# gMLP stage of a two-layer trunk: v ahead of u, the mixing matrix's two parts side by side, and the mixes between units of u

## The chip, the cores and the metric

The kernel runs on one core of a Trainium2 chip. The metric is the device time of one execution in microseconds (us). Of the kernel before, three runs took 1134.57 to 1136.39 us, with a median of 1135.93.

## The reference

The program computes a trunk of two layers on 512 tokens by 1024 channels: layer 0 mixes tokens by stick-breaking attention, layer 1 by a gated MLP, and each mixer is followed by a SwiGLU network (FFN). The change touches layer 1's mixer alone:

```
def token_mixing_mixer(h, w_in, ln_g, w_s, b_s, w_out):
    uv = jax.nn.gelu(h @ w_in)
    u, v = jnp.split(uv, 2, axis=-1)
    v = layer_norm(v, ln_g)
    ...
    ws = jnp.where(chunk_causal[None], w_s, 0.0).astype(v.dtype)
    sv = jnp.einsum('gts,bnsgc->bntgc', ws, v) + b_s.T[None, None, :, :, None]
    y = u * sv.reshape(B, S, D)
    return y @ w_out
```

There are 8 groups g of 128 channels, each with a mixing matrix of 128 positions by 128, and n counts 4 chunks of 128 tokens. So the mixing is 32 products of 128x128 by 128x128.

## The kernel before, in words

**Products in two parts.** A float32 operand is kept as a high part and a low part (`split`, L113: ScalarE rounds to the high part, VectorE subtracts for the low one). A product is three matmuls (`mm3`, L105): high by high, high by low, low by high, added up in one PSUM bank. A bank holds 128 x 512 float32. Six banks go round under one tag ("b"), and two more under a second one ("p").

**Order.** The PE's instructions run in the order in which the program was scheduled. Weights come as raw blocks of 512 KB through the SP queue, in the order of the list that `wadd` fills (L244); each is split into `wh` (ScalarE, L161) and `wl` (VectorE, L162) some units ahead of its use (`wget`, L235).

**Around the stage.** `out_proj` (L497) of FFN 0 ends in the boundary of each block of 128 tokens (`boundary`, L425): residual sum, two norms, 8 transposes on PE into `tp`, and the split into `hTh` and `hTl`, the transposed input of the next sub-layer. The transposes of blocks 2 and 3 must wait for a long chain on VectorE and ScalarE, so PE is given other work there: three closures `nxt`, of which the first runs before block 2's transposes, the second before block 3's, the third behind them. Before, these are `u_first` (L1324): units 0 and 1, units 2 and 3, and unit 4 of u, each for the first 256 tokens.

**The stage** (`gmlp`, L1331). A u unit m (`u_unit`, L1302) makes 128 channels of u for n tokens: 24 matmuls of 256 columns for 256 tokens, 48 for 512; ScalarE then applies GELU (L1315). v is made in two halves of 512 channels, each half in four banks (one for each token block), 24 matmuls of 512 columns a bank (L1345). In order:

1. load and split of the mixing matrices (`wsh`, `wsl`), load of the bias `bsb`; units 0 to 4 of u for tokens 256 to 511
2. v half 0, v half 1; into these `bg.step` deals out pieces of the next modulation's work (class `Bg`, L341), which end in 8 matmuls `adaps` with a matrix of ones, whose operand is split by ScalarE (`acch`) and VectorE (`accl`) just before
3. layer norm of v: statistics and normalising on VectorE, split into `vnh`, `vnl`; units 5 to 7 of u for all tokens stand on PE meanwhile
4. eight mixes (`mix`, L1393), one for each group: 12 matmuls of 128 columns into one bank `sv`, one VectorE instruction svt = sv * gain + bias of 512 columns, one u * svt, and the split of that product (`act_split`, L1043: `as` by ScalarE, then VectorE). From the fifth on, each is followed by `part(m - 4)` (L1415): 12 matmuls `y` of 512 columns, the output projection for token blocks 0 and 3, which take four banks
5. the rest of the projection, `out_proj` with its boundary

Of the kernel before, what the change touches and what calls it, by code (L numbers as in the profile page):

```python
# [13 lines left out]
P = 128  # L14
T = 512
# [16 lines left out]
def trunk(ctx: ExitStack, tc: tile.TileContext, A: dict, out: bass.AP):  # L32
# [21 lines left out]
    def slot(dt, name, a=2, b=512):  # L54
        return s4.tile([P, a, b], dt, tag="s4", name=nm(name))

    def bank(name, tag="b"):
        return psum.tile([P, 512], F32, tag=tag, bufs=6 if tag == "b" else 2, name=nm(name))
# [51 lines left out]
    def load(dst, src):  # L110
        nc.sync.dma_start(out=dst, in_=src)

    def split(hi, lo, src, hi_dve=False):  # L113
        if hi_dve:
            dve.tensor_copy(hi, src)
        else:
            act.activation(hi, src, AF.Copy)  # L117
        dve.tensor_tensor(lo, src, hi.bitcast(F32), ALU.subtract)
# [116 lines left out]
    def wget(src, look=3):  # L235

        n = taken[0]
        taken[0] += 1
        while len(got) < min(n + 1 + look, len(stream)):
            wemit()  # L240
        assert stream[n][3] == src, (stream[n][3], src)
        return got[n]

    def wadd(key, a, b, *idx):  # L244
        ap = A[key]
        stream.append((ap[idx], a, b, (key,) + idx))

    NH = 3
    NU = 5
    wadd("wv", 2, 512, 0, 0)  # L250
    wadd("wqk", 8, P, 0, 0)
    wadd("wqk", 8, P, 0, 1)
# [9 lines left out]
    for l in range(2):  # L262
        for f in range(NH):
            wadd("wgu", 8, P, l, f, 0)
            wadd("wgu", 8, P, l, f, 1)
        for f in range(NH, KF):
            stream.append((None, 0, 0, ("blocks", (l, f - NH))))
        if l == 1:
            for q in range(2):
                for p in PAIRS[q]:  # L270
                    wadd("wdn", 4, 256, q, p)
        if l == 0:
            for f in range(KF):
                wadd("wdown", 1, D, f)
            for m in range(NU):
                wadd("win_u", 8, P, m)
            for hf in range(2):
                for j in range(4):
                    wadd("win_v", 2, 512, hf, j)
            for m in range(NU, KD):  # L280
                wadd("win_u", 8, P, m)
            for k in range(KD):
                wadd("wout", 1, D, k)
# [1018 lines left out]
    def u_unit(hT, m, lo, n, w):  # L1302
        ub = bank("u")
        for k in range(KD):
            for c in range(0, n, 256):
                h, l = hB(hT, k, lo + c, 256)
                mm3(
                    ub[:, c : c + 256], w[0][:, k, :], w[1][:, k, :], h, l,
                    k + c == 0, k == KD - 1,
                )  # L1310

        def evac():
            if m // 2 == len(u4):
                u4.append(slot(F32, "u"))
            last_act[0] = act.activation(  # L1315
                u4[m // 2][:, m % 2, lo : lo + n], ub[:, :n], AF.Gelu_apprx_tanh
            )

        return evac

    uw = {}
    STEPS = 2

    def u_first(hT, ms):  # L1324
        ev = []
        for m in ms:
            uw[m] = wget(("win_u", m), 1)
            ev.append(u_unit(hT, m, 0, 256, uw[m]))
        return lambda: [e() for e in ev]

    def gmlp(bg, hT, nhT, nS, nxt):  # L1331
        wsr = wraw.tile([P, KD, P], F32, tag="raw", name="wsr")
        load(wsr[:], A["ws"])
        nc.gpsimd.memset(wsr[0:64, :, 64:P], 0.0)
        wsh = slot(F32R, "wsh", KD, P)
        wsl = slot(F32R, "wsl", KD, P)
        split(wsh[:], wsl[:], wsr[:])
        bsb = slot(F32, "bsb", KD, P)
        load(bsb[:].rearrange("p a b -> p (a b)"), A["bs"].to_broadcast([P, D]))
        for m in range(NU):  # L1340
            u_unit(hT, m, 256, 256, uw[m])()
        vt = [slot(F32, "vt", 1, 1024) for _ in range(NT)]
        vn = []

        def v_mm(vb, tt, k, w):  # L1345
            a, b = hB(hT, k, tt * P, P)
            mm3(vb[tt][:], a, b, w[0][:, k % 2, :], w[1][:, k % 2, :], k == 0, k == KD - 1)

        def v_gelu(vb, tt, hf):
            act.activation(  # L1350
                vt[tt][:, 0, hf * 512 : (hf + 1) * 512], vb[tt][:], AF.Gelu_apprx_tanh
            )

        vb = [bank("v") for _ in range(NT)]
        for k in range(KD):
            if k % 2 == 0:
                wv = wget(("win_v", 0, k // 2))
            for tt in range(NT):
                v_mm(vb, tt, k, wv)
            bg.step(STEPS)  # L1360
        for tt in range(NT):
            v_gelu(vb, tt, 0)
        vb = [bank("v") for _ in range(NT)]
        for k in range(4):
            if k % 2 == 0:
                wv = wget(("win_v", 1, k // 2))
            for tt in range(NT):
                v_mm(vb, tt, k, wv)
            bg.step(STEPS)
        bg.step(99)  # L1370
        tail = [wget(("win_v", 1, j)) for j in (2, 3)]
        st = small.tile([P, NT, 2, 6], F32, tag="bns", bufs=1, name=nm("bns"))
        mv = small.tile([P, NT, 2], F32, tag="mv", bufs=1, name=nm("mv"))
        for tt in range(NT):
            for k in range(4, KD):
                v_mm(vb, tt, k, tail[k // 2 - 2])
            v_gelu(vb, tt, 1)
            for hf in range(2):
                dve.bn_stats(st[:, tt, hf, :], vt[tt][:, 0, hf * 512 : (hf + 1) * 512])
            dve.bn_aggr(mv[:, tt, :], st[:, tt, :, :])  # L1380
        sd = small.tile([P, 52], F32, tag="sd4", bufs=1, name=nm("sd4"))[:, :NT]
        act.activation(sd, mv[:, :, 1], AF.Sqrt, bias=epsb[:])
        r = small2.tile([P, 48], F32, tag="r4", bufs=1, name=nm("r4"))
        dve.reciprocal(r[:, :NT], sd)
        for tt in range(NT):
            dve.tensor_scalar(
                vt[tt][:, 0, :], vt[tt][:, 0, :], mv[:, tt, 0:1], r[:, tt : tt + 1],
                ALU.subtract, ALU.mult,
            )
            vn.append((slot(F32R, "vnh", 1, 1024), slot(F32R, "vnl", 1, 1024)))  # L1390
            split(vn[tt][0][:, 0, :], vn[tt][1][:, 0, :], vt[tt][:, 0, :])

        def mix(m):  # L1393
            um = u4[m // 2][:, m % 2, :]
            sv = bank("sv")
            for n in range(NT):
                mm3(
                    sv[:, n * P : (n + 1) * P],
                    vn[n][0][:, 0, m * P : (m + 1) * P], vn[n][1][:, 0, m * P : (m + 1) * P],
                    wsh[:, m, :], wsl[:, m, :], True, True,  # L1400
                )
            t = fpool.tile([P, 768], F32, tag="e", name=nm("svt"))[:, :T]
            dve.scalar_tensor_tensor(
                t.rearrange("p (n t) -> p n t", n=NT),
                sv[:].rearrange("p (n t) -> p n t", n=NT), lng[:, m : m + 1],
                bsb[:, m : m + 1, :].to_broadcast([P, NT, P]), ALU.mult, ALU.add,
            )
            dve.tensor_tensor(um, um, t, ALU.mult)

        for m in range(NU, KD):  # L1410
            u_unit(hT, m, 0, T, wget(("win_u", m)))()
        sp = []
        pre = {"w": [], "y": {0: [None, None], 3: [None, None]}}

        def part(k):  # L1415

            w = wget(("wout", k), 2)
            pre["w"].append(w)
            for tt, y in pre["y"].items():
                for hf in range(2):  # L1420
                    if k == 0:
                        y[hf] = bank("y", "p" if tt == 3 else "b")
                    c = slice(hf * 512, (hf + 1) * 512)
                    tok = slice(tt * P, (tt + 1) * P)
                    mm3(
                        y[hf][:], sp[k][0][:, tok], sp[k][1][:, tok],
                        w[0][:, 0, c], w[1][:, 0, c], k == 0, False,
                    )

        for m in range(KD):  # L1430
            mix(m)
            sp.append(act_split(u4[m // 2][:, m % 2, :]))
            if m >= 4:
                part(m - 4)
        out_proj(
            2, KD, lambda k: sp[k], lambda k: ("wout", k), 4, bg, nhT, nxt, pre, nS,
        )
# [9 lines left out]
    bg2 = Bg("A2", "B2", lag=1, gap=3)  # L1447
    f0.run(
        Bg("G1", slots=1), Bg("A1", "B1", "G2"), bg2, 2, hT2,
        [lambda a=a: u_first(hT2, range(a, min(a + 2, NU))) for a in range(0, NU, 2)],  # L1450
    )
    gmlp(bg2, hT2, hT3, S3, f1.first())
    f1.last(Bg("G3", slots=1))
# [101 lines left out]
```

## Time and profile before

| what | us |
|---|---|
| median of three runs (range) | 1135.93 (1134.57 to 1136.39) |
| the profiled execution's own time | 1133.95 |
| its span | 1132.2 |
| PE busy (share of span) | 1110.9 (98%) |
| weight loads on PE | 999.9 (88%) |
| VectorE busy | 933.0 (82%) |
| ScalarE busy | 596.6 (53%) |
| the stage: first transposes of block 3 to the first boundary of its output | 643.85 to 768.71 |

Times within the execution count from the span's start. The profile names an instruction by its line, its engine, and output<-inputs by the program's names. A matmul's bar on PE is longer than the time it takes from its neighbours, since matmuls overlap: the distance from start to start is what a matmul costs. The mean granted clock of TensorE was 0.998.

### The profile page before, as it was taken

How to read it: one execution, taken by the hardware profiler on the slowest of the kernel's cores; microseconds unless marked ns; L12 is line 12 of the kernel's file. 1: busy time of each engine (PE TensorE's matmuls, PEld its weight loads, DVE VectorE, ACT ScalarE, POOL GpSimd, SP SyncE). 2: the span in 40 equal slices, each digit the busy share in tenths (PEclk: the TensorE clock that was granted, in tenths of full speed). 3: DMA queues.
4: the chain of work that ended last, by engine and by line, in shares of the span. 5: the costliest groups of instructions: out<-in, count | busy, mean ns of one | idle time of the engine just before them, and what ended most of it. 6: DMA issues, size and time to landing. Idle time of an engine off the chain costs nothing.

```text
span 1132.2 us, 18659 instructions
## 1 busy us (share of the span) xinstructions
PE 1110.9 (98%) x7436; PEld 999.9 (88%) x7436; DVE 933.0 (82%) x1223; ACT 596.6 (53%) x985; POOL 29.5 (3%) x53
## 2 busy tenths in 40 slices
PE   6999999999999999999999999999999999999997
PEld 4787878788999999998888988988999999999996
DVE  4988999958989898778686865759979898789996
ACT  6445655656655555572153624537455555465752
POOL 0120100000000000010000100001000000000000
PEclk9999999999999999999999999999999999999999
DMA  8876434214344343348886483324243434223242
GB/s 322 336 238 213 147 98 134 93 59 158 122 150 131 128 151 117 129 136 310 269 275 218 150 280 110 131 94 160 83 132 115 164 130 146 70 85 99 90 154 106
DMA packets 51356, 176.39 MB, mean 156 GB/s; under 512 B 6074, under 2 KB 9146, under 8 KB 51268
## 3 DMA queue, kind: packets, MB, share of 16 engines
q1 hardware_dynamic: 48708, 166.81, 43.6%
q0 software_dynamic: 2560, 8.39, 2.0%
q8 instruction: 58, 0.95, 0.3%
q14 instruction: 30, 0.25, 0.1%
HBM read 164.69 MB, written 8.39 MB: 153 GB/s over the span
## 4 chain that ended last, share of the span: by engine, by line
PE 88%; DVE 5%; ACT 3%; DMA 2%; issue 1%; SPq 0%; DVEq 0%; ACTq 0%
PE r L94 32%; PE y L94 16%; PE v L94 8%; PE pqk L94 7%; PE X L94 4%; PE gu L94 4%; PE Y L94 3%; PE u L94 3%; PE av L94 2%; PE z L94 2%; PE tw L102 1%; PE Z L94 1%; PE W L94 1%; PE tp L102 1%; PE ab L94 1%
## 5 line engine op out<-in xcount | busy, mean ns | idle before, releaser
L94 PE MATMUL r<-Sh,wl 128*128 128x256 f32 x608 | 170.0, 280 | 0.0
L94 PE MATMUL r<-Sh,wh 128*128 128x256 f32 x608 | 169.9, 279 | 0.0
L94 PE MATMUL r<-Sl,wh 128*128 128x256 f32 x608 | 169.8, 279 | 0.0
L161 ACT ACTIVATE wh<-raw 128x1024 fp32r<-128x1024 f32 x87 | 91.6, 1059 | 113.3 <-PE y L94 57.5
L94 PE MATMUL y<-wh,as 128*128 128x512 f32 x480 | 150.7, 391 | 0.0
L117 ACT ACTIVATE wh<-f 128x1024 fp32r<-128x1024 f32 x87 | 92.3, 1061 | 91.3 <-PE r L94 66.4
L70 DVE TENSOR_TENSOR wl<-f,wh 128x1024 fp32r<-128x1024 f32 x87 | 106.4, 1222 | 38.9 <-ACT wh L117 38.8
L162 DVE TENSOR_TENSOR wl<-raw,wh 128x1024 fp32r<-128x1024 f32 x87 | 105.8, 1221 | 38.2 <-ACT wh L161 37.5
L94 PEld LDWEIGHTS r<-Sl,wh 128*128 128x128 f32 x608 | 114.2, 188 | 0.0
L94 PEld LDWEIGHTS r<-Sh,wl 128*128 128x128 f32 x608 | 114.2, 188 | 0.0
L94 PEld LDWEIGHTS r<-Sh,wh 128*128 128x128 f32 x608 | 114.1, 188 | 0.0
L94 PEld LDWEIGHTS y<-wh,as 128*128 128x128 f32 x480 | 90.1, 188 | 18.6
L94 PE MATMUL y<-wl,as 128*128 128x512 f32 x240 | 93.8, 391 | 0.0
L94 PE MATMUL r<-hTh,wh 128*128 128x256 f32 x304 | 88.9, 293 | 0.6 <-DVE gu L70 0.6
L94 PE MATMUL r<-hTl,wh 128*128 128x256 f32 x304 | 84.8, 279 | 0.0
L94 PE MATMUL r<-hTh,wl 128*128 128x256 f32 x304 | 80.0, 279 | 0.0
L94 PEld LDWEIGHTS r<-hTh,wh 128*128 128x128 f32 x304 | 57.0, 188 | 5.9 <-DVE gu L70 2.4
L94 PE MATMUL r<-hTh,b 128*128 128x256 f32 x304 | 59.8, 279 | 0.0
L117 ACT ACTIVATE wh<-rawx 128x1024 fp32r<-128x1024 f32 x38 | 40.3, 1061 | 33.4 <-PE r L94 30.8
L94 PEld LDWEIGHTS r<-hTl,wh 128*128 128x128 f32 x304 | 57.2, 188 | 0.1
L94 PEld LDWEIGHTS r<-hTh,wl 128*128 128x128 f32 x304 | 55.0, 188 | 0.0
L94 PE MATMUL gu<-hTh,wh 128*128 128x256 f32 x192 | 54.0, 281 | 0.0
(272 smaller groups left out, 2960.7 us busy)
## 6 DMA issues: line engine op xcount, KB each, us to landing
rawada<-in_ada SPq DMA_DIRECT2D x80, 512.0 KB, 4.9
rawy<-in_wy SPq DMA_DIRECT2D x38, 512.0 KB, 3.5
rawx<-in_wx SPq DMA_DIRECT2D x38, 512.0 KB, 4.1
raw<-in_wdown SPq DMA_DIRECT2D x22, 512.0 KB, 4.6
raw<-in_wdn SPq DMA_DIRECT2D x22, 512.0 KB, 3.5
raw<-in_wqk SPq DMA_DIRECT2D x16, 512.0 KB, 4.5
ada<-in_ada0p SPq DMA_DIRECT2D x12, 512.0 KB, 9.0
raw<-in_wgu SPq DMA_DIRECT2D x12, 512.0 KB, 3.5
```

What stands on the lines that cost most here:

```text
L70: b = getattr(nc.vector, op)(*args, **kw)
L94: b = nc.tensor.matmul(o, l, r, start=start, stop=stop, skip_group_check=True)
L102: last_tp[0] = nc.tensor.transpose(o, i, ident)
L117: act.activation(hi, src, AF.Copy)
L161: act.activation(h[:], raw[:], AF.Copy)
L162: last_low[0] = nc.vector.tensor_tensor(l[:], raw[:], h[:].bitcast(F32), ALU.subtract)
```

## The change

**v first.** The work given to the boundary is now v half 0 for tokens 0 to 255 (two closures, 24 matmuls of 512 columns each) and unit 0 of u for the same tokens. `gmlp` begins with v half 0 for token blocks 2 and 3, then unit 0's second half, v half 1, the layer norm, and units 1 to 7 of u for all tokens. The loads of the mixing matrices and the bias move to the middle of v half 1. The list of raw blocks is put into the new order.

**Side by side.** High and low part of each mixing matrix stand next to each other in `ws`. One matmul of 256 columns makes v's high part by both; one of 128 columns adds v's low part by the high one. The two results lie 128 columns apart and are added by VectorE. A chunk takes 256 columns of a bank, so a mix takes two banks, 8 matmuls, and four VectorE instructions of 256 columns where there was one of 512.

**Mixes dealt out.** Mixes 0 to 3 stand behind units 4 to 7 of u, each followed by `bg.step(5)`, which moves the `adaps` matmuls there; mixes 4 to 7 each come with their `part`, as before.

```
-            for m in range(NU):
-                wadd("win_u", 8, P, m)
-            for hf in range(2):
-                for j in range(4):
-                    wadd("win_v", 2, 512, hf, j)
-            for m in range(NU, KD):
+            for j in range(4):
+                wadd("win_v", 2, 512, 0, j)
+            wadd("win_u", 8, P, 0)
+            for j in range(4):
+                wadd("win_v", 2, 512, 1, j)
+            for m in range(1, KD):
                 wadd("win_u", 8, P, m)
...
+    def v_first(hT, js):
+        if not v0:
+            v0["b"], v0["w"] = [bank("v") for _ in range(2)], []
+        for j in js:
+            w = wget(("win_v", 0, j), 1)
+            v0["w"].append(w)
+            for k in (2 * j, 2 * j + 1):
+                for tt in range(2):
+                    v_mm(hT, v0["b"], tt, k, w)
...
     def gmlp(bg, hT, nhT, nS, nxt):
...
+        vb = [None, None] + [bank("v") for _ in range(2)]
         for k in range(KD):
-            if k % 2 == 0:
-                wv = wget(("win_v", 0, k // 2))
-            for tt in range(NT):
-                v_mm(vb, tt, k, wv)
-            bg.step(STEPS)
-        for tt in range(NT):
+            for tt in (2, 3):
+                v_mm(hT, vb, tt, k, v0["w"][k // 2])
+            bg.step(1)
+        u_unit(hT, 0, 256, 256, v0["u"])()
...
+        ws = [slot(F32R, "ws", 4, 2 * P) for _ in range(2)]
+        for i, w in enumerate(ws):
+            split(w[:, :, 0:P], w[:, :, P:], wsr[:, 4 * i : 4 * i + 4, :])
...
         def mix(m):
             um = u4[m // 2][:, m % 2, :]
-            sv = bank("sv")
-            for n in range(NT):
-                mm3(
...
+            for b in range(2):
+                sv = bank("sv")
+                for i in range(2):
+                    vh, vl = [a[:, 0, mc] for a in vn[2 * b + i]]
+                    mm(sv[:, 256 * i : 256 * i + 256], vh, w, True, False)
+                    mm(sv[:, 256 * i : 256 * i + P], vl, w[:, 0:P], False, True)
+                s = sv[:].rearrange("p (n e t) -> p n e t", n=2, e=2)
+                dve.scalar_tensor_tensor(
+                    tv[:, b], s[:, :, 0, :], lng[:, m : m + 1],
+                    bsb[:, m : m + 1, :].to_broadcast([P, 2, P]), ALU.mult, ALU.add,
                 )
...
+                dve.scalar_tensor_tensor(
+                    tv[:, b], s[:, :, 1, :], lng[:, m : m + 1], tv[:, b], ALU.mult, ALU.add
+                )
             dve.tensor_tensor(um, um, t, ALU.mult)
...
-        for m in range(KD):
+        def mixed(m):
             mix(m)
             sp.append(act_split(u4[m // 2][:, m % 2, :]))
-            if m >= 4:
-                part(m - 4)
+
+        for m in range(1, KD):
+            u_unit(hT, m, 0, T, wget(("win_u", m)))()
+            if m > 3:
+                mixed(m - 4)
+                bg.step(5)
+        bg.step(99)
+        for m in range(4, KD):
+            mixed(m)
+            part(m - 4)
```

PE before, the first mix, right behind unit 7 of u (`sv` is the mix's bank; 12 rows a mix):

```order
L94 MATMUL sv_7363<-wsh_6677,vnh_7175 128x128
L94 MATMUL sv_7363<-wsl_6678,vnh_7175 128x128
L94 MATMUL sv_7363<-wsh_6677,vnl_7176 128x128
L94 MATMUL sv_7363<-wsh_6677,vnh_7180 128x128
L94 MATMUL sv_7363<-wsl_6678,vnh_7180 128x128
L94 MATMUL sv_7363<-wsh_6677,vnl_7181 128x128
```

PE in the change, the first mix and what follows it, behind unit 4 of u (`u_7201` is unit 5; `adaps` are the matmuls with ones):

```order
L94 MATMUL sv_7161<-ws_6824,vnh_6915 128x256
L94 MATMUL sv_7161<-ws_6824,vnl_6916 128x128
L94 MATMUL sv_7161<-ws_6824,vnh_6920 128x256
L94 MATMUL sv_7161<-ws_6824,vnl_6921 128x128
...
L94 MATMUL adaps_7179<-acch_6805,ones 128x512
L94 MATMUL adaps_7179<-accl_6806,ones 128x512
L94 MATMUL u_7201<-hTh_6310,wh_6992 128x256
L94 MATMUL u_7201<-hTl_6311,wh_6992 128x256
L94 MATMUL u_7201<-hTh_6310,wl_6993 128x256
L94 MATMUL u_7201<-hTh_6498,wh_6992 128x256
L94 MATMUL u_7201<-hTl_6499,wh_6992 128x256
L94 MATMUL adaps_7187<-acch_7183,ones 128x512
```

Six rows of 128 columns have become four, two of them with 256. The second pair of `adaps` stands five u matmuls behind the first; 21 u matmuls lie between its own two, and behind mix 1, in unit 6, it is the same with 12.

VectorE before, the first mix, and then in the change:

```order
L70 SCALAR_TENSOR_TENSOR svt_7376<-sv_7363,cols,bsb_6681 128x512
L70 TENSOR_TENSOR u_6666<-u_6666,svt_7376 128x512
L70 TENSOR_TENSOR as_7379<-u_6666,as_7379 128x512
L70 SCALAR_TENSOR_TENSOR svt_7395<-sv_7382,cols,bsb_6681 128x512
L70 TENSOR_TENSOR u_6666<-u_6666,svt_7395 128x512
```

```order
L70 SCALAR_TENSOR_TENSOR svt_7160<-sv_7161,cols,bsb_6830 128x256
L162 TENSOR_TENSOR wl_7361<-raw_7358,wh_7360 128x1024
L70 SCALAR_TENSOR_TENSOR svt_7160<-sv_7161,cols,svt_7160 128x256
L70 SCALAR_TENSOR_TENSOR svt_7160<-sv_7168,cols,bsb_6830 128x256
L70 SCALAR_TENSOR_TENSOR A_6071<-adaps_7179,g_6803 128x512
L70 SCALAR_TENSOR_TENSOR svt_7160<-sv_7168,cols,svt_7160 128x256
L70 TENSOR_TENSOR accl_7184<-A_6071,acch_7183 128x512
L70 TENSOR_TENSOR u_6620<-u_6620,svt_7160 128x512
```

One instruction of 512 columns has become four of 256, and a weight split and the work on `adaps` have come between them.

In the boundary PE had, counted in rows, 48 u matmuls, block 2's transposes, 49 u matmuls, block 3's transposes, and 23 u matmuls before the first one that needs block 3. It now has 24 of v, the transposes, 24 of v and 6 of u, the transposes, and 18 of u.

More of the change, by code (lines that the diff above doesn't have):

```diff
@@ L248, in trunk @@
     NH = 3
-    NU = 5
     wadd("wv", 2, 512, 0, 0)
@@ L1319, in u_unit @@
         return evac
-    uw = {}
     STEPS = 2
[L1324 to L1329, printed above, removed]
-    def gmlp(bg, hT, nhT, nS, nxt):
[L1332 to L1354, printed above, removed]
-        for k in range(KD):
-            if k % 2 == 0:
-                wv = wget(("win_v", 0, k // 2))
-            for tt in range(NT):
-                v_mm(vb, tt, k, wv)
-            bg.step(STEPS)
-        for tt in range(NT):
@@ new lines, in trunk, with v_mm, v_gelu @@
+    vt, v0 = {}, {}
+    def v_mm(hT, vb, tt, k, w):
+        a, b = hB(hT, k, tt * P, P)
+        mm3(vb[tt][:], a, b, w[0][:, k % 2, :], w[1][:, k % 2, :], k == 0, k == KD - 1)
+    def v_gelu(vb, tt, hf):
+        if tt not in vt:
+            vt[tt] = slot(F32, "vt", 1, 1024)
+        last_act[0] = act.activation(
+            vt[tt][:, 0, hf * 512 : (hf + 1) * 512], vb[tt][:], AF.Gelu_apprx_tanh
+        )
[8 more added lines that the diff above has]
+                    v_mm(hT, v0["b"], tt, k, w)
+        return lambda: [v_gelu(v0["b"], tt, 0) for tt in range(2) if 3 in js]
@@ L1362, in gmlp, with u_first @@
+    def u_first(hT):
+        v0["u"] = wget(("win_u", 0), 1)
+        return u_unit(hT, 0, 0, 256, v0["u"])
+    def gmlp(bg, hT, nhT, nS, nxt):
+        vb = [None, None] + [bank("v") for _ in range(2)]
+        for k in range(KD):
+            for tt in (2, 3):
+                v_mm(hT, vb, tt, k, v0["w"][k // 2])
+            bg.step(1)
+        u_unit(hT, 0, 256, 256, v0["u"])()
+        for tt in (2, 3):
             v_gelu(vb, tt, 0)
@@ L1367, in gmlp @@
             for tt in range(NT):
-                v_mm(vb, tt, k, wv)
+                v_mm(hT, vb, tt, k, wv)
             bg.step(STEPS)
-        bg.step(99)
+        wsr = wraw.tile([P, KD, P], F32, tag="raw", name="wsr")
+        load(wsr[:], A["ws"])
+        nc.gpsimd.memset(wsr[0:64, :, 64:P], 0.0)
+        ws = [slot(F32R, "ws", 4, 2 * P) for _ in range(2)]
+        for i, w in enumerate(ws):
+            split(w[:, :, 0:P], w[:, :, P:], wsr[:, 4 * i : 4 * i + 4, :])
+        bsb = slot(F32, "bsb", KD, P)
+        load(bsb[:].rearrange("p a b -> p (a b)"), A["bs"].to_broadcast([P, D]))
         tail = [wget(("win_v", 1, j)) for j in (2, 3)]
@@ L1375, in gmlp @@
             for k in range(4, KD):
-                v_mm(vb, tt, k, tail[k // 2 - 2])
+                v_mm(hT, vb, tt, k, tail[k // 2 - 2])
             v_gelu(vb, tt, 1)
@@ L1384, in gmlp @@
         dve.reciprocal(r[:, :NT], sd)
+        vn = []
         for tt in range(NT):
@@ L1394, in mix @@
             um = u4[m // 2][:, m % 2, :]
-            sv = bank("sv")
-            for n in range(NT):
-                mm3(
-                    sv[:, n * P : (n + 1) * P],
-                    vn[n][0][:, 0, m * P : (m + 1) * P], vn[n][1][:, 0, m * P : (m + 1) * P],
-                    wsh[:, m, :], wsl[:, m, :], True, True,
-                )
[L1402 to L1407, printed above, removed]
+            w = ws[m // 4][:, m % 4, :]
+            t = fpool.tile([P, 768], F32, tag="e", name=nm("svt"))[:, :T]
+            tv = t.rearrange("p (b n t) -> p b n t", b=2, n=2)
+            mc = slice(m * P, (m + 1) * P)
+            for b in range(2):
[8 more added lines that the diff above has]
+                    bsb[:, m : m + 1, :].to_broadcast([P, 2, P]), ALU.mult, ALU.add,
+                )
+                dve.scalar_tensor_tensor(
+                    tv[:, b], s[:, :, 1, :], lng[:, m : m + 1], tv[:, b], ALU.mult, ALU.add
+                )
             dve.tensor_tensor(um, um, t, ALU.mult)
-        for m in range(NU, KD):
-            u_unit(hT, m, 0, T, wget(("win_u", m)))()
         sp = []
@@ L1449, in trunk @@
         Bg("G1", slots=1), Bg("A1", "B1", "G2"), bg2, 2, hT2,
-        [lambda a=a: u_first(hT2, range(a, min(a + 2, NU))) for a in range(0, NU, 2)],
+        [lambda: v_first(hT2, (0, 1)), lambda: v_first(hT2, (2, 3)), lambda: u_first(hT2)],
     )
```

## The prediction

> **What bounds the kernel now.** I read the page's busy times first, then the chain of waits through the stage, then the waits of PE.
>
> ```profile
> PE 1110.9 (98%) x7436; PEld 999.9 (88%) x7436; DVE 933.0 (82%) x1223; ACT 596.6 (53%) x985; POOL 29.5 (3%) x53
> ```
>
> PE is busy for 98%, so what it is given to do decides, unless something makes it wait. The chain of the stage (start, us, what):
>
> ```profile
> 643.85 1.10 PE tp L102 x8
> 644.95 16.85 PE u L94 x143
> 661.80 24.64 PE v L94 x108
> 686.44 0.47 PE adaps L94 x2
> ...
> 689.65 0.58 PE adaps L94 x2
> ...
> 707.68 16.96 PE u L94 x144
> 724.64 6.65 PE sv L94 x60
> 731.29 2.81 PE y L94 x12
> 734.11 1.29 PE sv L94 x12
> 735.39 2.83 PE y L94 x12
> 738.23 1.29 PE sv L94 x12
> 739.51 2.83 PE y L94 x12
> 742.35 1.29 PE sv L94 x12
> 743.63 25.04 PE y L94 x110
> ```
>
> It never leaves PE: from 643.85 to 768.68 every piece is a matmul. So in this stage a matmul saved is time saved, until another engine falls behind. The one wait at its edge stands at the transposes of block 3; the number in brackets is PE's idle time and who ended it:
>
> ```profile
> 636.79 1.03 PE L102 MATMUL tp<-identt,t 128*128 128x128 f32 x8
> ...
> 643.31 0.28 PE L94 MATMUL u<-hTh,wh 128*128 128x256 f32 x1
> 643.85 1.10 PE L102 MATMUL tp<-identt,t 128*128 128x128 f32 x8 [0.26 <-DVE t L70]
> ```
>
> **The costs per matmul**, from counts and lengths of the chain: u (256 columns) 16.96 / 144 = 0.118 us, v (512 columns) 24.64 / 108 = 0.228, sv (128 columns) 6.65 / 60 = 0.111. The start times show the step from u to sv:
>
> ```profile
> 724.25 0.28 PE L94 MATMUL u<-hTl,wh 128*128 128x256 f32 x1
> 724.37 0.28 PE L94 MATMUL u<-hTh,wl 128*128 128x256 f32 x1
> 724.48 0.22 PE L94 MATMUL sv<-wsh,vnh 128*128 128x128 f32 x1
> 724.54 0.27 PE L94 MATMUL sv<-wsl,vnh 128*128 128x128 f32 x1
> 724.65 0.28 PE L94 MATMUL sv<-wsh,vnl 128*128 128x128 f32 x1
> 724.76 0.27 PE L94 MATMUL sv<-wsh,vnh 128*128 128x128 f32 x1
> ```
>
> One gap, 724.48 to 724.54, is 0.06: half the columns of u, half of u's step. The next are 0.11, almost what 256 columns cost. So a matmul of 128 columns is not paid by its columns here. I read it as each matmul waiting for its weights, of which 128 x 128 are loaded for every one; then a mix is paid by its matmuls.
>
> **Term 1, the mixes on PE.** 96 matmuls become 64. Before, the chain gives 6.65 + 3 x 1.29 = 10.52 us. After, 32 of 256 columns and 32 of 128: at 0.111 each 7.1, and at 0.118 for the wider ones 7.3. That saves 3.2 to 3.4; I take **-3.3**. If columns were what counts, nothing would be saved, since 96 x 128 = 32 x 256 + 32 x 128; that is a rival below.
>
> **Term 2, the boundary.** Nothing is added to u or v; they change places. Between block 2's transposes (636.79, before) and block 3's stood 49 u matmuls, 5.78 us. Now it is 24 of v and 6 of u, 5.47 + 0.71 = 6.18, and ahead of block 2's transposes 24 of v, 5.47, where 48 of u took 5.66. So PE reaches block 3's transposes 0.4 - 0.19 = 0.2 us later than it did, against an idle time of 0.26. The instruction that makes `t` is VectorE's:
>
> ```profile
> 642.52 1.28 DVE L70 SCALAR_TENSOR_TENSOR t<-t,r,B 128x1024 f32<-128x1024 f32 x1
> ```
>
> It ends at 643.80, behind a weight split as before, for the new order has as many raw blocks here. So most of 0.26 goes: **-0.25**, from 0 (if `t` moves with it) to -0.3. What is late next is the split of block 3: 18 u matmuls (2.1 us) cover it now, not 23 (2.7).
>
> ```profile
> 644.55 1.09 ACT L117 ACTIVATE hTh<-tp 128x512 fp32r<-128x512 f32 x2 [0.66 <-PE tp L102]
> 645.18 1.29 DVE L70 TENSOR_TENSOR hTl<-tp,hTh 128x512 fp32r<-128x512 f32 x2 [1.38 <-ACT hTh L117]
> ```
>
> It is done at 646.47. Transposes ending at 644.95 and 18 u matmuls lead to 647.0: covered by 0.5; without that cover, up to 0.6 is paid.
>
> **Term 3, adaps among units 5 and 6.** The 8 matmuls with ones are the same in number. But between the first pair and the next operand's use stood 12 v matmuls (686.90 to 689.65, 2.7 us), and now there are 5 of u, 0.59. A PE instruction that waits holds all behind it. ScalarE has the split of a raw block, a GELU and the operand's split to do behind the end of the unit, in the lengths and order of these rows:
>
> ```profile
> 724.56 1.06 ACT L161 ACTIVATE wh<-raw 128x1024 fp32r<-128x1024 f32 x1 [4.06 <-PE u L94]
> 725.53 0.58 ACT L1315 ACTIVATE u<-u 128x512 f32<-128x512 f32 x1
> ...
> 690.65 0.62 ACT L117 ACTIVATE acch<-B 128x512 fp32r<-128x512 f32 x1
> ```
>
> From the unit's last matmul (start 724.37) to the end of the operand: 0.19 + 0.97 + 0.58 + 0.62 = 2.36, less some overlap of neighbours (0.1 each), 2.2. PE has 8 sv, 2 adaps and 5 u to do in that time: 0.9 + 0.47 + 0.59 = 1.96. So it stands for some 0.3, twice (units 5 and 6). The pair at 689.65 took 0.58 where that at 686.44 took 0.47, so 0.1 was lost there before. I take **+0.5**, from 0 (ScalarE has taken the raw block earlier) to 1.2 (VectorE's part is late as well).
>
> **Term 4, VectorE in the mixes.** What is removed and added for one mix, by these rows:
>
> ```profile
> L70 DVE SCALAR_TENSOR_TENSOR svt<-sv,cols,bsb 128x512 f32<-128x512 f32 x8 | 6.0, 746 | 0.0
> L70 DVE SCALAR_TENSOR_TENSOR ar<-tw,ar 128x384 fp32r<-128x384 f32 x32 | 16.3, 552 | 2.6 <-ACT ar L918 2.4
> L70 DVE SCALAR_TENSOR_TENSOR ar<-tw,ar 128x512 fp32r<-128x512 f32 x16 | 10.3, 684 | 5.1 <-ACT ar L918 5.1
> L70 DVE TENSOR_TENSOR u<-W,u 128x256 f32<-128x256 f32 x12 | 4.3, 418 | 0.0
> L70 DVE TENSOR_TENSOR u<-u,svt 128x512 f32<-128x512 f32 x8 | 5.5, 692 | 0.3
> ```
>
> The trace has no such instruction with 256 columns. From 384 to 512 columns the price rises by 132 ns, 1.03 ns a column; taking 256 columns off 746 gives 480 ns. The bounds are 418 (a simpler instruction of 256 columns) and 746 (no cheaper than the whole); 480 is near the lower one, and I take it. VectorE's work for a mix is then 4 x 0.48 + 0.69 + 0.69 = 3.3 us, where it was 2.1. PE's step with a `part` is 0.9 + 2.83 = 3.7, so VectorE keeps up, and mixes 0 to 2 lie beside units of u of 48 x 0.118 = 5.7 us. The narrow place is behind unit 7: mixes 3 to 7, five, take VectorE 5 x 3.3 = 16.5 us, and PE 5 x 0.9 + 4 x 2.83 = 15.8. The banks that hold mix 7 are wanted again, for the projection, some 17.2 us behind unit 7, and by 480 ns VectorE frees them at 16.6. Slack 0.6, so **0**. It is gone at about 0.52 us an instruction; each further 0.1 us on some 17 instructions costs 1.7 us.
>
> **What stays at nothing.** The layer norm's chain had 17 us of u beside it (707.68 to 724.64) and gets four units, 22.6. The raw blocks come three units ahead at 5.7 us a unit, and one lands in 4.7:
>
> ```profile
> raw<-in_win_u SPq DMA_DIRECT2D x8, 512.0 KB, 4.7
> ```
>
> The mixing matrices' load is moved behind v's blocks on SP's queue, and has the second part of v half 1 and four units, over 30 us, before its use. Without this cover a late block would cost up to 4.7 us.
>
> **The sum.** -3.3 - 0.25 + 0.5 + 0 = -3.05. The profiled execution took 1133.95 (span 1132.2) and would take 1130.9. It lies 2 us under the median of the runs; on the median of 1135.93 the forecast is **1132.9**.
>
> **A rule of the Trainium skill against it.** The trace's 0.11 us step of 128 columns is at odds with one rule. The Trainium skill, "TensorE: Matmul & The Clock Gate", section "Back-to-back issue gap", gives an isolated warm matmul N/2.4 + 2.5 ns, 56 ns for 128 columns and 109 for 256; by that page I estimate 5.4 us for the 96 before and 5.3 for the 64 after, so the sum would come to 1136.2 like the first rival below. The same page's section "LDWEIGHTS (loading the stationary operand)" gives P/1.2 ns, 107 for 128 columns, and this is what the steps of 0.111 agree with.
>
> **The rivals.** *Columns count (6%).* PE streams a mix's columns and the 0.111 is a matter of this row of instructions. For it: the one step of 0.06. Against: 59 others. Then term 1 is 0, and the time 1135.93 - 0.25 + 0.5 = 1136.2.
>
> *VectorE holds the banks, mildly (15%).* The strided reads of every second 128 columns in PSUM make a half as dear as 0.69. For it: svt's 746 lies above the 684 of `ar` with the same columns. Against: 418 for 256 columns. It costs (0.69 - 0.52) x 17 = 2.9, and gives 1135.8; PE would stand before the first `y` behind mix 7.
>
> *VectorE holds the banks, slower (7%).* The same place at a price of 0.95, twice the estimate, for example if the second of two, which reads what the first wrote, has to wait for it. It costs (0.95 - 0.52) x 17 = 7.3, and gives 1140.2. It decides from 0.83 on, where the loss passes 3.05 + 2.27. Against: the rows of VectorE that read what their predecessor wrote show no such gap (u<-u,svt behind svt, 0.3 us idle in eight).
>
> That the mix is not changed as said is excluded by the order of the rows: there are 64 in place of 96.
>
> **Chances.** This kernel's measurement can tell 0.2%, 2.27 us, from no change: faster is below 1133.66, slower above 1138.20. My case has 72%; its own range is 1131.9 (no stall at adaps, all else good) to 1134.5 (1.2 there, and the split of block 3 not covered), and I put 62 of the 72 below 1133.66. Columns and mild VectorE, 21%, end within 0.2%; with 10 of my case that is 31. Slower 7%. The range reaches down to 1131.3, for a boundary or adaps better than their rows, and up to 1136.5 to take in both middle cases; it leaves out the slower one and a little on either side.
>
> **What would show it.** sv: 64 matmuls with steps of 0.11 to 0.12 and some 7.2 us in all (term 1). The transposes of block 3 without a wait on `t` (term 2). Two waits of PE at `adaps` for `acch`, 0.2 to 0.4 each (term 3). VectorE's svt instructions of 256 columns near 0.48 us and no wait of PE before `y` (term 4). I am wrong if PE's waits for svt or u appear in the mixes, or if 256 columns of sv cost 0.2.

## The result, and the profile after

The changed kernel took **1132.67 us** (median of 18 runs, 1129.73 to 1135.34) beside 1136.16 of the kernel before (18 runs, 1132.41 to 1140.69). The ratio is **0.9967** with a 95% interval of 0.9955 to 0.9979: faster by 0.33%, 3.7 us, within 2.4 and 5.1. Forecast were 1132.9 and a gain of 3.05.

The busy times on the page of the changed kernel:

```profile
PE 1110.1 (98%) x7404; PEld 997.3 (88%) x7404; DVE 940.2 (83%) x1248; ACT 596.7 (53%) x982; POOL 29.6 (3%) x53
```

PE has 32 matmuls fewer, VectorE 25 instructions more and 7 us more to do. This execution took 1135.34 us, more than the 1133.95 of the one before, and yet the stage got shorter. To see it, both must be measured from a mark inside. I take the stretch from block 1's transposes in FFN 0's boundary to block 0's in the next one. Timeline of PE, first before, then after:

```profile
626.32 1.06 PE L102 MATMUL tp<-identt,t 128*128 128x128 f32 x8
...
768.71 1.09 PE L102 MATMUL tp<-identt,t 128*128 128x128 f32 x8
```

```profile
630.77 1.06 PE L102 MATMUL tp<-identt,t 128*128 128x128 f32 x8
...
648.19 1.06 PE L102 MATMUL tp<-identt,t 128*128 128x128 f32 x8
...
769.54 1.09 PE L102 MATMUL tp<-identt,t 128*128 128x128 f32 x8
```

The stretch went from 142.39 to **138.77** us, by -3.62. The execution after came to its first mark 4.45 us later, in a part of the program where nothing was changed. Of these, 3.0 us had arisen 48 us into the program, half of them while the granted clock was at 0.50 to 0.75 (36 to 40 us); in the execution before it was 1.00 there. So two profiled times say nothing on 3 us here, and two stretches do; these agree to some 0.2 us (see "The sum" below). The transposes of block 3 (648.19) have no wait in brackets any more. The chain of waits after:

```profile
648.23 1.02 PE tp L102 x8
649.25 2.12 PE u L94 x18
651.37 10.89 PE v L94 x48
...
686.85 22.61 PE u L94 x192
709.46 0.88 PE sv L94 x8
710.35 0.00 issue
710.35 0.58 ACT u L1314
710.92 0.53 ACT acch L117
711.46 0.04 issue
711.50 0.50 PE adaps L94
712.00 2.47 PE u L94 x21
...
731.70 1.80 PE sv L94 x16
733.50 2.82 PE y L94 x12
736.32 0.87 PE sv L94 x8
737.19 2.79 PE y L94 x12
...
743.64 0.87 PE sv L94 x8
744.51 25.00 PE y L94 x110
```

A mix is 0.87 to 0.90 us where it was 1.29. The chain leaves PE once in these rows, for ScalarE at 710.35 (and once more, behind mix 1). It is the wait at `adaps`; the timeline of PE's weight loads has it twice, 0.28 us each:

```profile
711.50 0.19 PEld L94 LDWEIGHTS adaps<-acch,ones 128*128 128x128 f32 x1 [0.28 <-ACT acch L117]
...
719.32 0.19 PEld L94 LDWEIGHTS adaps<-acch,ones 128*128 128x128 f32 x1 [0.28 <-ACT acch L117]
```

Inside a mix the starts look like this:

```profile
709.30 0.28 PE L94 MATMUL sv<-ws,vnh 128*128 128x256 f32 x1
709.41 0.22 PE L94 MATMUL sv<-ws,vnl 128*128 128x128 f32 x1
709.47 0.33 PE L94 MATMUL sv<-ws,vnh 128*128 128x256 f32 x1
709.64 0.22 PE L94 MATMUL sv<-ws,vnl 128*128 128x128 f32 x1
```

Past the first, a matmul of 256 columns is followed after 0.17 us and one of 128 after 0.06, 0.23 for the two. The weight loads in between start evenly, at 709.30, 709.42, 709.53, 709.65, 709.75 and 709.88, just as in the kernel before (724.37, 724.48, 724.59). So it is the loads that come every 0.11 us, whatever the width, and not the matmuls.

The groups of VectorE, by shape (busy us, mean ns of one, idle time before):

```profile
L70 DVE SCALAR_TENSOR_TENSOR svt<-sv,cols,bsb 128x256 f32<-128x256 f32 x16 | 7.3, 478 | 8.0 <-PE sv L94 8.0
L70 DVE SCALAR_TENSOR_TENSOR svt<-sv,cols,svt 128x256 f32<-128x256 f32 x16 | 7.3, 478 | 0.1
```

The half instruction takes 478 ns, and no row of PE's waits names svt: VectorE waits for PE, 8.0 us in all, and not PE for it.

### The profile page after: what moved, and what is told of

The parts are those of the page before. It is cut to its first block, busy times and chain, and to the rows that moved or that the text cites. A ratio compares the mean times of both kernels' runs of the same rounds, so it can differ in the third digit from the quotient of the medians.

```text
span 1133.6 us, 18637 instructions
## 1 busy us (share of the span) xinstructions
PE 1110.1 (98%) x7404; PEld 997.3 (88%) x7404; DVE 940.2 (83%) x1248; ACT 596.7 (53%) x982; POOL 29.6 (3%) x53
## 4 chain that ended last, share of the span: by engine, by line
PE 78%; DMA 8%; DVE 8%; ACT 3%; issue 2%; SPq 0%; POOL 0%; DVEq 0%; ACTq 0%
PE r L94 31%; PE y L94 9%; PE pqk L94 6%; PE v L94 5%; PE X L94 4%; PE u L94 4%; PE gu L94 4%; DMA rawada<-in_ada 4%; PE Y L94 3%; PE av L94 2%; PE z L94 2%; PE tw L102 1%; PE Z L94 1%; PE W L94 1%; PE tp L102 1%
```

## The experiments

The theory: the gain is that of the 32 mix matmuls saved, each paid by its weights; it is kept because units of u and the projection cover VectorE's four instructions a mix; the new order by itself is worth nothing. The rivals: it is the order that gains; columns are paid; VectorE is hidden in any order. What was measured, with the stretch from the traces (the "stage" of the first four expectations is this stretch less 4.81 us), the wait of PE at block 3's transposes in the next boundary, and times beside runs of the kernel before in the same sitting:

| kernel | stretch | that wait | median us (runs) | before | ratio (95%) |
|---|---|---|---|---|---|
| before | 142.39 | 0.81 | | | |
| changed | 138.77 | 1.35 | 1132.67 (18) | 1136.16 | 0.9967 (0.9955 to 0.9979) |
| e1, mix alone | 142.23 | 1.21 | 1135.05 (12) | 1135.45 | 0.9994 (0.9981 to 1.0007) |
| e2, order alone | 143.25 | 0.83 | 1137.38 (12) | 1135.45 | 1.001 (0.9997 to 1.0023) |
| e3, adaps in v | 140.01 | 1.18 | 1134.21 (12) | 1135.45 | 0.9994 (0.9982 to 1.0005) |
| e4, half the columns | 138.86 | 1.26 | 1134.2 (1) | 1135.45 | |
| e5, a pair a mix | 138.04 | 1.22 | 1130.81 (11) | 1134.91 | 0.9968 (0.9957 to 0.998) |
| e6, one more each | 139.14 | 1.06 | 1132.8 (1) | 1134.91 | |
| e7, two more each | 142.23 | 2.45 | 1137.63 (10) | 1134.91 | 1.0029 (1.0015 to 1.0042) |

### e1: the mix alone

In the kernel before, `wsh` and `wsl` become `ws`, and `mix` the one of the change; the order stays.

```
-        wsh = slot(F32R, "wsh", KD, P)
-        wsl = slot(F32R, "wsl", KD, P)
-        split(wsh[:], wsl[:], wsr[:])
+        ws = [slot(F32R, "ws", 4, 2 * P) for _ in range(2)]
+        for i, w in enumerate(ws):
+            split(w[:, :, 0:P], w[:, :, P:], wsr[:, 4 * i : 4 * i + 4, :])
```

> The mixes with both parts side by side (8 matmuls, four VectorE instructions) in the order of the kernel before: u first, all eight mixes behind unit 7. My theory (fewer matmuls pay 3.4 us, but VectorE's 3.3 us a mix must find cover in units of u): VectorE needs 8 x 3.3 = 26.4 us behind unit 7, and the projection's banks for blocks 1 and 2 are free only then, while PE has some 21 us of work that it may do; so PE waits 4 to 6 us, the gain is gone, and the stage (from the first matmul behind FFN 0's projection to the next boundary's first transposes; 137.6 us before, 134.0 after) takes 138 to 140 us, the time 1136 to 1139. Rival (the dealing out is not needed, the saved matmuls are saved in any order): stage 134.1, time 1132.7.

Stage 137.4 us, time the same as before: next to nothing of the 3.4 us is left, and the rival falls. The theory's sign was right, its sizes were not: PE waits 1.1 us behind unit 7 and not 4 to 6, and the stage is shorter than the 138 to 140 expected. Timelines of VectorE and PE in this kernel, behind unit 7 of u:

```profile
737.57 0.87 DVE L70 SCALAR_TENSOR_TENSOR svt<-sv,cols,bsb 128x256 f32<-128x256 f32 x2
738.35 0.69 DVE L70 TENSOR_TENSOR as<-u,as 128x512 fp32r<-128x512 f32 x1
738.96 0.87 DVE L70 SCALAR_TENSOR_TENSOR svt<-sv,cols,svt 128x256 f32<-128x256 f32 x2
739.75 0.68 DVE L70 TENSOR_TENSOR u<-u,svt 128x512 f32<-128x512 f32 x1
740.35 0.87 DVE L70 SCALAR_TENSOR_TENSOR svt<-sv,cols,bsb 128x256 f32<-128x256 f32 x2
```

```profile
728.37 0.36 PE L94 MATMUL sv<-ws,vnh 128*128 128x256 f32 x1 [0.53 <-DVE svt L70]
729.99 0.64 PE L94 MATMUL y<-wh,as 128*128 128x512 f32 x1 [0.51 <-ACT as L117]
```

VectorE without a gap does a mix in 740.35 - 737.57 = 2.78 us, not 3.3: an instruction that has 0.48 in the row starts 0.39 behind its predecessor. So it is less behind than I said, and PE's waits are short. But see the windows of PE (us, busy (count) of PE, PEld, DVE, ACT and POOL, then the granted clock, DMA share and GB/s):

```profile
727.00:728.00 1.00, 0.78 (x6) 0.53 (x4) 1.00 (x4) 0.18 (x1) 0.00 (x0) 1.00 0.30 61
728.00:729.00 1.00, 0.63 (x5) 0.66 (x6) 1.00 (x3) 0.00 (x0) 0.00 (x0) 1.00 0.90 246
729.00:730.00 1.00, 0.49 (x6) 0.34 (x4) 1.00 (x4) 0.63 (x1) 0.00 (x0) 1.00 0.97 389
730.00:731.00 1.00, 1.00 (x3) 0.81 (x4) 1.00 (x3) 0.00 (x0) 0.00 (x0) 0.59 0.86 352
731.00:732.00 1.00, 1.00 (x4) 0.81 (x3) 1.00 (x4) 0.00 (x0) 0.00 (x0) 0.50 0.00 0
732.00:733.00 1.00, 1.00 (x6) 0.91 (x6) 1.00 (x4) 0.63 (x1) 0.00 (x0) 0.50 0.00 0
733.00:734.00 1.00, 1.00 (x5) 0.82 (x5) 1.00 (x3) 0.00 (x0) 0.00 (x0) 0.70 0.00 0
```

From 727 to 730 PE lacks 0.22 + 0.37 + 0.51 = 1.1 us. Then it is busy again, but in these four windows the clock is 0.59, 0.50, 0.50 and 0.70, which by the clock alone is 0.41 + 0.50 + 0.50 + 0.30 = 1.7 us more; from 734 on it has 1.00 again. The waits and the lowered clock together are 2.8 us, most of the 3.5 saved. That the waits brought the clock down is not shown: other waits were not followed by this (see the last section).

### e2: the order alone

In the changed kernel, `ws` and `mix` are again those of the kernel before (the diff of e1 the other way round).

> The new order (v ahead, mixes behind units 4 to 7, adaps there) with the mixes of the kernel before: 12 matmuls of 128 columns into one bank, one VectorE instruction. My theory: the order alone is worth about nothing: -0.25 at the boundary, +0.5 at adaps; mixes 10.5 us, stage 137.4 to 137.9, time 1136.2, the same as before. Rival (the gain is the order's: v in long matmuls gives covers that u did not): stage 134 to 136, time 1133 to 1134.5.

Stage 138.4, a little above the theory's 137.9, and the rival falls: the order by itself gains nothing and loses 0.9 us. Two waits of 0.5 at `adaps`, for VectorE's `accl`, are the loss; the boundary has no wait (644.20, 17.40 us behind block 1's transposes, as in the changed kernel). By times it is not told from no change.

### e3: adaps in v

```
             for tt in (2, 3):
                 v_mm(hT, vb, tt, k, v0["w"][k // 2])
-            bg.step(1)
+            bg.step(STEPS)
...
             bg.step(STEPS)
+        bg.step(99)
         wsr = wraw.tile([P, KD, P], F32, tag="raw", name="wsr")
```

> The changed kernel with the next modulation's steps dealt out to v again, two a step and the rest behind the fourth, so that the adaps matmuls stand in v half 1 and not among units 5 and 6. My theory: the two waits of 0.28 us go, nothing takes their place, stage 133.4 (134.0 in the changed kernel), time 0.5 us below it, which the runs can hardly tell. Rival (ScalarE and VectorE are the later ones wherever adaps stands, since each operand's split waits for the one before): the waits come back in v half 1, stage 134.0 or more.

The rival was right. The two waits are gone, and one of 1.38 has come in their place, in v half 1 (and a small one, 0.26 at the weight load of another `adaps`, for `acch`). PE and VectorE there:

```profile
668.51 0.50 PE L94 MATMUL adaps<-accl,ones 128*128 128x512 f32 x1 [1.38 <-DVE accl L70]
```

```profile
665.36 0.68 DVE L70 SCALAR_TENSOR_TENSOR A<-adaps,g 128x512 f32<-128x512 f32 x1
666.57 1.28 DVE L70 SCALAR_TENSOR_TENSOR B<-rawada,sc,B 128x1024 f32<-128x1024 f32 x1 [0.53 <-DMA rawada<-in_ada]
667.77 0.68 DVE L70 TENSOR_TENSOR accl<-A,acch 128x512 fp32r<-128x512 f32 x1
```

`accl` stands behind a step that waits for its block from the DMA: a wait on one engine is paid on the other. The stretch is 1.24 us longer than the changed kernel's. By its times (0.9994) this kernel is not told from no change, although its stretch is 2.4 us below that of the kernel before; 0.4 of that goes in the next boundary's wait, and the 2.0 left are 0.18%, at the edge of the interval.

### e4: half the columns

The product of v's high part by the mixing matrix's low part is left out; 64 matmuls of 128 columns stay.

```
-                    mm(sv[:, 256 * i : 256 * i + 256], vh, w, True, False)
-                    mm(sv[:, 256 * i : 256 * i + P], vl, w[:, 0:P], False, True)
+                    mm(sv[:, 256 * i : 256 * i + P], vh, w[:, 0:P], True, True)
+                    mm(sv[:, 256 * i + P : 256 * i + 256], vl, w[:, 0:P], True, True)
```

> The changed kernel, but every mix matmul has 128 columns: high by low of the mixing matrix is left out, so the number of matmuls stays at 64 and the columns go from 12288 to 8192. My theory (a mix matmul is paid by its weights, not by its columns): sv takes 7.1 us in all as in the changed kernel, and the stage 134.0. Rival (columns are paid): 32 x 0.06 = 1.9 us less, sv 5.2 and the stage 132.1.

The theory holds. In the chain a mix takes 0.84 to 0.86 us where the changed kernel has 0.87 to 0.89, so a third of the columns is worth 0.03 us a mix, and the stretch is the same within 0.1. The rival's 1.9 us are not there.

### e5: one pair of adaps behind each mix

```
             if m > 3:
                 mixed(m - 4)
-                bg.step(5)
+                bg.step(3)
```

> The changed kernel with bg.step(3) in place of bg.step(5) behind mixes 0 to 3, so that one pair of adaps matmuls stands behind each of the four mixes and none among u; each operand is split a whole unit of u (5.7 us) ahead of its use. My theory (the two waits of 0.28 us come from an operand that is split right before its use, behind the weight split and the GELU on ScalarE): no wait of PE on acch or accl is left, the stretch from block 1's transposes of FFN 0's boundary to block 0's of the next boundary takes 138.2 us (138.77 in the changed kernel), time 0.5 us below the changed kernel's. Rival (the operands wait for VectorE's or the DMA's part wherever they stand, as they did in v): waits of 0.3 us or more on accl, 138.8 or more.

The chain of this kernel at mix 0; mixes 1 to 3 read alike:

```profile
705.58 0.87 PE sv L94 x8
706.45 0.51 PE adaps L94 x2
706.96 5.65 PE u L94 x48
```

No wait at `adaps` is left in the stage, and the stretch is 138.04, 0.73 below the changed kernel's (0.6 expected). It is the shortest of all. By its times (0.9968) it is not told from the changed kernel (0.9967).

### e6 and e7: where VectorE becomes the bound

The first instruction of each half is done two and three times; the repeats write the same values.

```
-                dve.scalar_tensor_tensor(
-                    tv[:, b], s[:, :, 0, :], lng[:, m : m + 1],
-                    bsb[:, m : m + 1, :].to_broadcast([P, 2, P]), ALU.mult, ALU.add,
-                )
+                for _ in range(2):
+                    dve.scalar_tensor_tensor(
+                        tv[:, b], s[:, :, 0, :], lng[:, m : m + 1],
+                        bsb[:, m : m + 1, :].to_broadcast([P, 2, P]), ALU.mult, ALU.add,
+                    )
```

> The changed kernel with the first VectorE instruction of each half of a mix done twice (the second writes the same values), so six of 256 columns a mix in place of four. Theory from the trace (back to back one costs 0.395 us and a u * svt 0.6, so a mix is 2.78 us of VectorE, and 3.57 here): below PE's 3.7 a mix, banks free just in time, no wait or one under 0.3; the stretch 138.8 us. Rival (they cost 0.48 and 0.69 back to back, as the prediction had it, 4.3 us a mix here): VectorE frees mix 7's banks about 3 us late, the stretch 142 us.

> The same instruction done three times, eight of 256 columns a mix. Theory (0.395 us each, a mix 4.36 us of VectorE, above PE's 3.7): five mixes take 21.8 us and free the last banks some 3.5 us late; PE waits 3 to 4 us in the mixes, the granted clock falls behind the waits as it did in the kernel with the mixes alone, and the stretch takes 142 to 144.5 us, the time 1136 to 1138.5. Rival (VectorE is hidden by u and the projection whatever it does): 138.8.

With six instructions a mix the stretch is 0.4 us longer (139.14), and the chain shows 0.06 of waiting ahead of a `y` (at 748.07); so the price back to back is the one that holds, and 0.48 is refuted. With eight it is 3.5 us longer (142.23), as much as the whole gain, and the kernel is slower than before (1.0029). PE waits for svt there, but once and for 0.49, not for 3 to 4:

```profile
736.42 0.35 PE L94 MATMUL sv<-ws,vnh 128*128 128x256 f32 x1 [0.49 <-DVE svt L70]
```

Another 1.28 us of the 3.5 is a wait at the end of the stretch, at block 0's transposes (772.22). The chain leads back from there over weight blocks that e7 requests from 757.90 on and the changed kernel from 752.40 on. What is left is not lost: PE's order in e7 is another, in which four `sv` and some `y` take turns, as they do in e1, and 154 matmuls `y` stand between unit 7 and the mark where the changed kernel has 147 (7 x 0.227 = 1.6 us). How much of the late blocks is due to VectorE and how much to that order was not separated. Behind the mark the wait at block 3's transposes is 2.45 where it was 1.35. The granted clock stayed at 1.00 in the mixes, where it was expected to fall, and fell behind this last wait: 0.54, 0.50, 0.50 and 0.76 from 801 to 805, another 1.7 us.

## Why the prediction was right, point by point

- **Term 1, -3.3.** Right. The mixes took 10.52 us and take 0.88 + 0.89 + 0.87 + 1.80 + 3 x 0.87 = 7.05: -3.47. e4 shows why: the number of matmuls counts, not the columns. That it counts by the weight loads is read from the traces: loads start 0.11 apart in both kernels, while matmuls start 0.06 and 0.17 apart by turns, so it is not a fixed price for each matmul's start. No run changed the loads alone. The sign "steps of 0.11 to 0.12" thus holds as a mean (0.23 for two) and not for each step.
- **Term 2, -0.25.** Right. The wait of 0.26 at block 3's transposes is gone, and 18 u matmuls covered the split behind them: the chain goes on from 649.25 without a break.
- **Term 3, +0.5.** Right in place and cause: two waits of 0.28 for `acch`, behind the weight split and the GELU on ScalarE. e5, without them, is 0.73 shorter, so they cost at least what was forecast.
- **Term 4, 0.** Right in the sum, mis-sized in the working. 480 ns was forecast for the half instruction and 478 measured, but I added up lengths. Neighbours overlap, and start to start it is 0.39, a u * svt 0.60: 2.78 us a mix and not 3.3. So VectorE was not 0.04 us an instruction from being the bound, as I said: 6 x 0.39 + 1.2 = 3.5 us a mix still fits PE's 3.7 (e6), and 8 x 0.39 + 1.2 = 4.3 does not (e7). The "slower" rival would have needed about twice the work, which e7 is; e7 did come out slower, but not where that rival put the loss: PE's only wait for svt was 0.49, so e7 shows that eight are too many and not that the banks are what is late. The timeline of VectorE before showed the overlap already; the second row starts 0.60 behind one of 0.69:

```profile
729.03 0.69 DVE L70 TENSOR_TENSOR as<-u,as 128x512 fp32r<-128x512 f32 x1 [0.76 <-ACT as L117]
729.63 0.75 DVE L70 SCALAR_TENSOR_TENSOR svt<-sv,cols,bsb 128x512 f32<-128x512 f32 x1
```

- **The sum.** -3.05 was forecast. The stretch shows -3.62, of which -0.2 is that 192 v matmuls stand 0.227 apart (10.89 / 48) and not 0.228 (24.64 / 108). That is no effect of the change: e1, with v as in the kernel before, has the 0.227 as well, so 0.2 is what two stretches can differ by of themselves. Behind the stretch the wait at block 3's transposes in the next boundary has grown by 0.54 (0.81 to 1.35), which the prediction did not have. Together -3.1, inside the interval of the runs. The terms leave some 0.3 us of the stretch unassigned. So the mechanism was right, and that the total is met to 0.1 us is partly luck: -0.5 that no term had and the +0.54 cancel.
- **Columns count.** Refuted by e4. What the Trainium skill, "TensorE: Matmul & The Clock Gate", section "Back-to-back issue gap", gives for an isolated matmul is not what a mix pays here; the 0.11 of the section on LDWEIGHTS is. The first of these sections says itself that its figure under-counts where the columns are few, since it leaves the weight load out, so the rule was less at odds with the trace than the prediction made it. Its sum by that page should read 1136.1 and not 1136.2, as 5.4 less 5.3 is a gain of 0.1.

What stays open: the growth by 0.4 us of the wait in the next boundary. It is there in all seven kernels with the new mix (1.06 to 1.35; 2.45 in e7) and not in the two with the old one (0.81, 0.83). The chain leads to a weight block:

```profile
783.94 5.15 DMA raw<-in_wgu
789.09 0.02 issue
789.11 1.06 ACT wh L161
```

Two blocks are requested one right behind the other in every kernel. In the kernel before this row reads 783.10 4.65, with the request as far behind block 0's transposes (14.39 us there, 14.40 here); so the growth is the block's own 0.5 us on the way. Why it takes longer behind the new mix was not tried.

## What to carry to other kernels

Where matmuls with few columns stand 0.11 us apart whatever their width, make them wider and fewer: two products of 128 columns with the same stationary operand (the one that is loaded as weights) side by side cost about one. It ends somewhere above 256 columns: at 512 a matmul took 0.227. The sums that PE no longer makes move to VectorE, so look for a place where VectorE is covered: the same mix gained 3.6 us dealt out between units of u and nothing in one piece (e1). And price a busy engine from start to start of neighbours in a row, not by the lengths of the rows.

## What the runs showed of the hardware

- The granted clock fell in the same way in five places: each time some 1.7 us were lost over four windows of 1 us, the middle ones at 0.50. In e1 this stood behind three gaps of PE of 0.2 to 0.5 us within 3 us, in e7 behind a wait of 2.45, and in the changed kernel, e4 and e7 behind a wait of 1.05 to 1.10 at 35 to 37 us.
- The length of a wait does not decide it. That last wait stands at the same place in all nine kernels (1.04 to 1.10), and in the other six the clock stayed at 1.00 behind it. Two waits of 0.28 some 8 us apart (changed kernel), two of 0.5 (e2), one of 1.38 (e3) and 0.5 us within 2 us (e7) were followed by no drop either. What decides was not tried. The Trainium skill, "TensorE: Matmul & The Clock Gate", section "A second HAM failure mode: psum-queue depth-cycling", tells of short idle times between groups of matmuls, while they cycle through PSUM banks, that send the clock to half and back. e1's 0.50 agrees; the waits of the other kernels show that not each of them does it.
- The same program comes to the same mark up to 4.6 us apart (618.93 to 623.53 for block 0's transposes in FFN 0's boundary, over the kernels here, which are alike up to there). The three that come last, at 622.73 and later, are those in which the clock fell at 36 us. Changes of 1 us are read from stretches between marks.
